# FFN down projection in 1024-column products with seven products for some pairs, and the residual kept in DRAM

## The chip, the cores and the metric

The kernel runs on one core of one Trainium2 chip, in one launch. The metric is device time in microseconds (us) of that core, the median of several runs. TensorE (PE in the profile) multiplies, VectorE (DVE), ScalarE (ACT) and GpSimd (POOL) work elementwise, SyncE (SP) issues most transfers.

## The reference

One layer of a block for 256 tokens of width 2048: RMSNorm, a combined input projection, latent attention and differential attention, gated merge, output projection, and then the part that the change concerns, a SwiGLU feed-forward network (FFN) with a hidden width of 5632 and the final norm. All tensors are float32.

```python
x = x + merged @ w_out[i]
h2 = rmsnorm(x, ffn_norm_g[i])
x = x + (jax.nn.silu(h2 @ w_ffn_gate[i]) * (h2 @ w_ffn_up[i])) @ w_ffn_down[i]
return rmsnorm(x, final_norm_g)
```

## The kernel before

Each float32 operand is split into a high part in float32r and the rest, also in float32r (`split`, L92 a cast on ScalarE, L93 a subtraction on VectorE). A product of two split operands takes three matmuls, high x high, high x low, low x high (`mm3`, L176 to L178), each 128 rows of k by 128 tokens by up to 512 columns. The 256 tokens are two halves h of 128. Weights are loaded from DRAM in pieces of 128 x 2 x 512 (tile raw, six buffers, on SP's queue), split into tiles w (eight buffers) or t (five), and used once. Activations are kept transposed, in tiles L (48 buffers); scratch tiles are s (eight buffers) and n (four).

The output projection runs in four chunks of 512 columns. Each chunk adds x to the product (L593), keeps the sum as the residual x2 in SBUF (eight L tiles until the end), and transposes it (L601) into h2T, the operand of the FFN. For the pairs of k-blocks in SEVEN = (0, 2, 4) `sums_of` also makes h2S, four sums and differences of the pair's four 128 x 128 blocks.

The FFN's 11 hidden chunks of 512 columns go in three parts, of 4, 4 and 3 chunks. `hidden(c, between)` multiplies h2T by 512 gate and 512 up columns over eight pairs of k-blocks. A plain pair takes 8 block products, 24 matmuls. A pair in SEVEN is done in the manner of Strassen and Winograd: `seven_weights` forms sums of the weight blocks (L645 to L647) and splits them, seven block products (21 matmuls) go into PSUM banks 1 to 7, and after the last such pair VectorE and ScalarE combine banks 1, 5, 6 and 7 into four base tiles (L699 to L703). Banks 2, 3, 4 and 8 go on accumulating; at the chunk's end the bases are added to them (L723, L724), and silu and the product with up follow (L726, L727). `between()` is called ahead of pair 6 and transposes the hidden chunk before into banks 5 and 6 (L677), split into fT.

After the hidden chunks of a part its down projection runs, in four chunks of 512 columns, all plain: two banks each, (1, 7) and (2, 3) in turn, accumulated over the part's 16 or 12 k-blocks. The part's last hidden chunk is transposed (`behind()`) ahead of the last four k-blocks of chunk 0. At each chunk's end the two banks are added to x2 (L762). In the last part chunks 0 to 2 are also squared and summed (L244) and multiplied by the final gain, and chunk 3 comes last, its half h=1 in two column halves; after it the row factors are worked out and the rows scaled and stored.

The order of instructions on each engine is set at build time by a scheduler that replays the program against its own clock; on the chip each engine's queue is in order. So neighbouring matmuls can belong to different chunks.

Of the kernel before, what the change touches and what calls it, by code (L numbers as in the profile page):

```python
# [8 lines left out]
F32 = mybir.dt.float32  # L9
# [5 lines left out]
P = 128  # L15
# [23 lines left out]
def hybrid_block(ctx: ExitStack, tc: tile.TileContext, x, xT, gains, w_lat, w_kr, w_dqk, w_dv, w_g0, w_g1, b_gate,  # L39
# [531 lines left out]
    def sums_of(tp, gs):  # L571

        a, t = nt((P, 2, S)), nt((P, 4, P))
        for j in range(2):
            nc.scalar.activation(out=a[:, j], in_=tp[:, j], func=AF.Copy, scale=gs[j])
        a11, a12, a21, a22 = a[:, 0, 0:P], a[:, 1, 0:P], a[:, 0, P:S], a[:, 1, P:S]
        nc.vector.tensor_tensor(out=t[:, 0], in0=a21, in1=a22, op=ALU.subtract)
        nc.vector.tensor_tensor(out=t[:, 1], in0=a11, in1=a21, op=ALU.subtract)
        nc.vector.tensor_tensor(out=t[:, 2], in0=t[:, 0], in1=a11, op=ALU.subtract)
        nc.vector.tensor_tensor(out=t[:, 3], in0=a12, in1=t[:, 2], op=ALU.add)  # L580
        hi, lo = lt(F32R, (P, 4, P)), lt(F32R, (P, 4, P))
        split(t, hi, lo)
        return hi, lo

    x2ss = const.tile([P, 8], F32, name="x2ss")
    for c in range(4):
# [9 lines left out]
        x2.append(z)  # L596
# [64 lines left out]
    def seven_products(q, pair, w, start, stop):  # L661

        hi, lo = h2S[pair]
        s1, s3, s2, s4 = [(hi[:, j], lo[:, j]) for j in range(4)]
        a0, a1 = h2T[2 * pair], h2T[2 * pair + 1]
        ls = {1: part_of(a0, 0), 2: part_of(a1, 0), 3: s4, 4: part_of(a1, 1), 5: s1, 6: s2, 7: s3}
        for i in (1, 5, 7, 6, 2, 3, 4) if start else (1, 3, 2, 5, 7, 6, 4):
            mm3(q[i], ls[i], w[i], start, stop and i in (1, 5, 6, 7))

    def transposed(f, alloc=lt, roles=(5, 6)):  # L670

        res = []
        for i, role in enumerate(roles):
            tp = bank(role, (P, 2, S))
            for j in range(2):
                for h in range(2):
                    nc.tensor.transpose(tp[:, j, h * P:(h + 1) * P], f[h][:, (2 * i + j) * P:(2 * i + j + 1) * P],  # L677
                                        ident)
            hi, lo = alloc(F32R), alloc(F32R)
            split(tp, hi, lo)  # L680
            res += [(hi[:, j], lo[:, j]) for j in range(2)]
        return res

    def hidden(c, between):

        pairs = len(h2T) // 2
        last = max(SEVEN) if SEVEN else None
        q, base = {}, None
        for p in range(pairs):
            if p == pairs - 2:  # L690
                between()
            if p in SEVEN:
                w = seven_weights(w_gu[c, p])
                if not q:
                    q = {i: bank(i) for i in (1, 5, 7, 6, 2, 3, 4)}
                seven_products(q, p, w, p == min(SEVEN), p == last)
                if p == last:
# [8 lines left out]
            g0_, u1, u0, g1_ = plain_weights(w_gu[c, p])  # L706
            if 8 not in q:
                q[8] = bank(8)
            if not SEVEN and not p:
                q.update({i: bank(i) for i in (2, 3, 4)})  # L710
            for a, (wg, wu) in ((h2T[2 * p], (g0_, u0)), (h2T[2 * p + 1], (g1_, u1))):
                first_k = a is h2T[0]
                for h, (i, j) in enumerate(((2, 3), (4, 8))):
                    l = part_of(a, h)
                    end = a is h2T[-1]
                    mm3(q[i], l, wg, first_k, end)
                    mm3(q[j], l, wu, first_k or (j == 8 and SEVEN and p == 1 and a is h2T[2]), end)
# [164 lines left out]
```

## Time and profile before

| | |
|---|---|
| runs, median (lowest to highest) | 1666.11 us (1664.88 to 1667.57), 3 runs |
| profiled execution | 1665.36 us, span in the profile 1663.6 us |
| PE, DVE, ACT, POOL busy | 99%, 70%, 51%, 2% of the span |
| TensorE's granted clock | 0.999 of full speed |
| HBM | 315.9 MB read, 6.3 MB written, 194 GB/s |

Times in the profile are us from the span's start unless marked ns. A busy share says how long an engine was occupied, not whether it set the time; matmuls overlap, so that their durations add up to more than the time that they take. Idle time is put down to what ended it.

### The profile page before, as it was taken

The page shows a single profiled execution, that of the slowest core. Times are in us where ns is not written, and L with a number is a line of the kernel's source. Part 1 is how long each engine was busy: PE and PEld are TensorE (multiplying, and loading weights), DVE is VectorE, ACT ScalarE, POOL GpSimd, SP SyncE. Part 2 cuts the span into 40 slices and gives each one's busy share as a digit, 9 for nine tenths or more (in the row PEclk, how much of TensorE's full clock was granted, in tenths as well). Part 3 has the DMA queues.
Part 4 walks back from the last instruction along what each step waited for, and adds up shares of the span by engine and source line. Part 5 has one row for each costly group of instructions (what it writes and reads, how often), then busy time and mean ns, then how long its engine had stood idle before and what let it go on. Part 6 is the DMA issues. An engine that isn't in the chain of part 4 may idle for free.

```text
span 1663.6 us, 22367 instructions
## 1 busy us (share of the span) xinstructions
PE 1648.0 (99%) x8443; PEld 1407.1 (85%) x8443; DVE 1158.8 (70%) x1490; ACT 845.2 (51%) x1158; POOL 26.2 (2%) x49
## 2 busy tenths in 40 slices
PE   8999999999999999999999999999999999999998
PEld 7888888888888999998888788888888888888886
DVE  7676665666555766765656889975679885688865
ACT  6465554455444666565445555544445554445543
POOL 0000000010000000000000000000000000000010
PEclk9999999999999999999999999999999999999999
DMA  9655555466666545556766566666566655566662
GB/s 329 222 176 168 175 176 178 153 197 203 213 209 197 180 159 176 169 170 207 237 213 207 176 192 197 206 202 202 190 202 202 199 189 196 186 203 203 197 221 103
DMA packets 99133, 323.67 MB, mean 195 GB/s; under 512 B 10960, under 2 KB 17104, under 8 KB 99024
## 3 DMA queue, kind: packets, MB, share of 16 engines
q1 hardware_dynamic: 98880, 322.22, 58.7%
q8 instruction: 66, 1.08, 0.3%
q14 instruction: 43, 0.35, 0.1%
q10 hardware_dynamic: 144, 0.02, 0.0%
HBM read 315.91 MB, written 6.29 MB: 194 GB/s over the span
## 4 chain that ended last, share of the span: by engine, by line
PE 97%; DMA 1%; DVE 1%; ACT 0%; issue 0%; SPq 0%; ACTq 0%; POOLq 0%; POOL 0%; DVEq 0%
PE q L176 14%; PE q L177 14%; PE q L178 14%; PE mm L176 12%; PE mm L177 12%; PE mm L178 12%; PE mm L201 9%; PE mm L202 5%; PE ps L178 1%; PE ps L177 1%; PE ps L176 1%; PE q L677 1%; PE ps L108 1%; DMA raw<-in_w_dqk_dram 1%; DMA raw<-in_w_gu_dram 0%
## 5 line engine op out<-in xcount | busy, mean ns | idle before, releaser
L93 DVE TENSOR_TENSOR wlo<-raw,whi 128x1024 fp32r<-128x1024 f32 (+3 forms) x320 | 381.8, 1194 | 258.1 <-ACT whi L92 252.8
L92 ACT CAST whi<-raw 128x1024 fp32r<-128x1024 f32 (+3 forms) x320 | 329.0, 1028 | 349.0 <-PE mm L177 250.9
L176 PE MATMUL mm<-whi,L 128*128 128x512 f32 (+2 forms) x1080 | 384.0, 358 | 4.7 <-ACT whi L92 4.7
L178 PE MATMUL mm<-whi,L 128*128 128x512 f32 (+2 forms) x1080 | 385.8, 358 | 0.0
L177 PE MATMUL mm<-wlo,L 128*128 128x512 f32 (+2 forms) x1080 | 385.3, 357 | 0.0
L177 PE MATMUL q<-w,L 128*128 128x512 f32 x900 | 350.3, 390 | 0.0
L178 PE MATMUL q<-w,L 128*128 128x512 f32 x900 | 350.0, 390 | 0.0
L92 ACT CAST w<-raw 128x1024 fp32r<-128x1024 f32 x192 | 198.9, 1052 | 262.2 <-PE q L177 254.3
L176 PE MATMUL q<-w,L 128*128 128x512 f32 x900 | 315.0, 390 | 0.3 <-DVE L L96 0.3
L93 DVE TENSOR_TENSOR w<-raw,w 128x1024 fp32r<-128x1024 f32 x192 | 231.7, 1220 | 108.7 <-ACT w L92 108.7
L201 PE MATMUL mm<-L,whi 128*128 128x512 f32 x672 | 240.1, 398 | 0.6 <-DVE n L211 0.6
L176 PEld LDWEIGHTS mm<-whi,L 128*128 128x128 f32 x1080 | 204.3, 190 | 32.8 <-ACT whi L92 4.7
L178 PEld LDWEIGHTS mm<-whi,L 128*128 128x128 f32 x1080 | 204.4, 189 | 28.4
L177 PEld LDWEIGHTS mm<-wlo,L 128*128 128x128 f32 x1080 | 204.4, 189 | 28.3 <-DVE wlo L93 0.5
L176 PEld LDWEIGHTS q<-w,L 128*128 128x128 f32 x900 | 168.8, 188 | 35.2 <-PE q L178 0.7
L178 PEld LDWEIGHTS q<-w,L 128*128 128x128 f32 x900 | 169.0, 188 | 34.9
L177 PEld LDWEIGHTS q<-w,L 128*128 128x128 f32 x900 | 169.0, 188 | 34.6
L202 PE MATMUL mm<-L,wlo 128*128 128x256 f32 x672 | 189.4, 282 | 0.0
L201 PEld LDWEIGHTS mm<-L,whi 128*128 128x128 f32 x672 | 126.2, 188 | 28.5 <-DVE n L211 0.9
L202 PEld LDWEIGHTS mm<-L,wlo 128*128 128x128 f32 x672 | 127.0, 189 | 0.7
L93 DVE TENSOR_TENSOR w<-t,w 128x1024 fp32r<-128x1024 f32 x66 | 79.6, 1218 | 4.6 <-ACT w L92 4.0
L92 ACT CAST w<-t 128x1024 fp32r<-128x1024 f32 x66 | 68.5, 1051 | 25.2 <-PE q L177 12.6
(190 smaller groups left out, 1368.7 us busy)
## 6 DMA issues: line engine op xcount, KB each, us to landing
raw<-in_w_gu_dram SPq DMA_DIRECT2D x176, 512.0 KB, 4.6
raw<-in_w_fd_dram SPq DMA_DIRECT2D x88, 512.0 KB, 4.1
raw<-in_w_dqk_dram SPq DMA_DIRECT2D x64, 512.0 KB, 3.3
raw<-in_w_g_dram SPq DMA_DIRECT2D x64, 512.0 KB, 3.3
raw<-in_w_diff_dram SPq DMA_DIRECT2D x32, 512.0 KB, 3.3
raw<-in_w_mla_dram SPq DMA_DIRECT2D x32, 512.0 KB, 4.0
raw<-in_w_out_dram SPq DMA_DIRECT2D x32, 512.0 KB, 3.7
raw<-in_w_dv_dram SPq DMA_DIRECT2D x30, 512.0 KB, 3.2
```

The costliest lines, as they stand in the source:

```text
L92: nc.scalar.copy(hi, src)
L93: nc.vector.tensor_tensor(out=lo, in0=src, in1=hi.bitcast(F32), op=ALU.subtract)
L108: nc.tensor.transpose(tp[:, j, h * P:(h + 1) * P], blk[h], ident)
L176: nc.tensor.matmul(o, lhsT=l[0], rhs=r[0], start=start, stop=False)
L177: nc.tensor.matmul(o, lhsT=l[0], rhs=r[1], start=False, stop=False)
L178: nc.tensor.matmul(o, lhsT=l[1], rhs=r[0], start=False, stop=stop)
L201: nc.tensor.matmul(o[b], lhsT=ws[k][0][:, bs], rhs=a, start=k == 0, stop=False)
L202: nc.tensor.matmul(o[b][:, :S], lhsT=ws[k][1][:, bs], rhs=ah, start=False, stop=k == len(aT) - 1)
L677: nc.tensor.transpose(tp[:, j, h * P:(h + 1) * P], f[h][:, (2 * i + j) * P:(2 * i + j + 1) * P], ident)
```

## The change

The down projection too goes in chunks of 1024 columns. A new function `product` does what `hidden` did inside, for either operand: n pairs of k-blocks against 1024 columns, pairs in `seven` by seven products, the others plainly, with banks 1, 5, 6, 7 for combined products and 2, 3, 4, 8 for the outputs. `hidden` calls it with h2T and h2S. In parts 0 and 1 the down projection is two products over eight pairs with three seven-product pairs each; in the last part it is one product over six pairs with two such pairs (columns 0 to 1023), then chunk 2 plainly in banks 1 and 7, then chunk 3 as before. `behind()` is called ahead of the last two pairs of a part's first product. For the pairs concerned `transposed` also makes the sums fS of the transposed hidden chunk. `w_ffn_down` is laid out accordingly on the host.

The residual x2 is stored to DRAM in the output projection (eight stores on SP's queue). In parts 0 and 1 base and bank are added and the sum is added to x2 in DRAM by an accumulating transfer issued from POOL (16 of them). In the last part x2 is loaded again (xf, eight loads, with the four rows of the final gain, on POOL's queue), and base and bank are added to it one after the other. The squares of chunks 0 to 2 are taken on ScalarE.

```diff
@@ -570,14 +570,17 @@
 
     def sums_of(tp, gs):
 
-        a, t = nt((P, 2, S)), nt((P, 4, P))
-        for j in range(2):
-            nc.scalar.activation(out=a[:, j], in_=tp[:, j], func=AF.Copy, scale=gs[j])
...
+        a, t = sc((P, 4, P)), sc((P, 4, P))
+        if gs is None:
+            nc.scalar.copy(a.rearrange("p a b -> p (a b)"), tp.rearrange("p a b -> p (a b)"))
+        else:
+            for j in range(2):
+                nc.scalar.activation(out=a[:, 2 * j:2 * j + 2].rearrange("p a b -> p (a b)"), in_=tp[:, j], func=AF.Copy,
+                                     scale=gs[j])
+
+        nc.vector.tensor_tensor(out=t[:, 0:2], in0=a[:, 0:2], in1=a[:, 1::2], op=ALU.subtract)
+        nc.vector.tensor_tensor(out=t[:, 2], in0=t[:, 1], in1=a[:, 0], op=ALU.subtract)
+        nc.vector.tensor_tensor(out=t[:, 3], in0=a[:, 2], in1=t[:, 2], op=ALU.add)
         hi, lo = lt(F32R, (P, 4, P)), lt(F32R, (P, 4, P))
         split(t, hi, lo)
         return hi, lo
@@ -593,7 +596,9 @@
             nc.vector.tensor_add(t, xr, o[h])
             square_sum(t, x2ss[:, 4 * h + c:4 * h + c + 1])
             z.append(t)
-        x2.append(z)
+        x2.append(dram.tile([P, 2, 512], F32, name=f"x2_{c}"))
+        for h in range(2):
+            nc.sync.dma_start(out=x2[c][:, h], in_=z[h])
...
@@ -658,43 +663,25 @@
...
+    def product(aT, aS, n, w, seven, at=None, between=None):
+
+
         q, base = {}, None
-        for p in range(pairs):
-            if p == pairs - 2:
+        outs = (2, 3, 4, 8)
+        for p in range(n):
+            if p == at:
                 between()
-            if p in SEVEN:
-                w = seven_weights(w_gu[c, p])
-                if not q:
-                    q = {i: bank(i) for i in (1, 5, 7, 6, 2, 3, 4)}
-                seven_products(q, p, w, p == min(SEVEN), p == last)
-                if p == last:
+            if p in seven:
+                ws = seven_weights(w(p))
+                fresh = 1 not in q
+                if fresh:
+                    q.update({i: bank(i) for i in (1, 5, 7, 6) + (() if p else outs[:3])})
+                s3, s1, s2, s4 = [(aS[p][0][:, j], aS[p][1][:, j]) for j in range(4)]
+                a0, a1 = aT[2 * p], aT[2 * p + 1]
+                ls = {1: part_of(a0, 0), 2: part_of(a1, 0), 3: s4, 4: part_of(a1, 1), 5: s1, 6: s2, 7: s3}
+                for i in (1, 5, 7, 6, 2, 3, 4) if fresh else (1, 3, 2, 5, 7, 6, 4):
+                    mm3(q[i], ls[i], ws[i], p == 0 if i in outs else fresh, i not in outs and p == max(seven))
+                if p == max(seven):
                     c1, v2, v3, d12, d22 = (sc() for _ in range(5))
                     nc.scalar.copy(c1, q[1])
                     nc.vector.tensor_tensor(out=v2, in0=c1, in1=q[6], op=ALU.add)
@@ -703,66 +690,95 @@
                     nc.vector.tensor_tensor(out=d22, in0=q[5], in1=v3, op=ALU.subtract)
                     base = ((c1, d12), (v3, d22))
                 continue
...
+            b11, b22, b12, b21 = plain_weights(w(p))
+            for k, bs in ((2 * p, (b11, b12)), (2 * p + 1, (b21, b22))):
+                for h in range(2):
+                    for i, b in zip(outs[2 * h:2 * h + 2], bs):
+                        start = i not in q
+                        if start:
+                            q[i] = bank(i)
+                        mm3(q[i], part_of(aT[k], h), b, start, k == 2 * n - 1)
+        return [[(base[h][v] if base else None, q[outs[2 * h + v]]) for v in range(2)] for h in range(2)]
+
+    def transposed(f, seven=False):
+
+        res, sums = [], None
+        for i in range(2):
+            tp = bank(5 + i, (P, 2, S))
+            for j in range(2):
+                for h in range(2):
+                    nc.tensor.transpose(tp[:, j, h * P:(h + 1) * P], f[h][:, (2 * i + j) * P:(2 * i + j + 1) * P],
+                                        ident)
+            if seven and not i:
+                sums = sums_of(tp, None)
+            hi, lo = lt(F32R), lt(F32R)
+            split(tp, hi, lo)
+            res += [(hi[:, j], lo[:, j]) for j in range(2)]
+        return res, sums
+
+    def hidden(c, between):
         f = []
+        for h, ((g_, gq), (u_, uq)) in enumerate(product(h2T, h2S, 8, lambda p: w_gu[c, p], SEVEN, 6, between)):
             sg = nt()
+            nc.vector.tensor_tensor(out=sg, in0=g_, in1=gq, op=ALU.add)
+            nc.vector.tensor_tensor(out=u_, in0=u_, in1=uq, op=ALU.add)
+            nc.scalar.activation(out=sg, in_=sg, func=AF.Silu, scale=r2[:, h:h + 1])
+            nc.vector.scalar_tensor_tensor(out=sg, in0=u_, scalar=r2[:, h:h + 1], in1=sg, op0=ALU.mult, op1=ALU.mult)
             f.append(sg)
         return f
     parts = ((0, 4), (4, 8), (8, 11))
     for i, (a, b) in enumerate(parts):
-        fT, f = [], None
+        fT, fS, f = [], {}, None
+        n = 2 * (b - a)
+        last = i == len(parts) - 1
+        seven = SEVEN[:2] if last else SEVEN
 
         def behind():
             if f:
-                fT.extend(transposed(f))
+                p = len(fT) // 2
+                t, sums = transposed(f, p in seven)
+                fT.extend(t)
+                fS[p] = sums
 
         for c in range(a, b):
             f = hidden(c, behind)
...
+        if last:
+            xf = []
+            for c in range(4):
+                xf.append([lt(shape=(P, 512)) for _ in range(3)])
+                for h in range(2):
+                    nc.gpsimd.dma_start(out=xf[c][h], in_=x2[c][:, h])
+                gf = xf[c][2]
+                nc.gpsimd.dma_start(out=gf, in_=final_norm_g[512 * c:512 * c + 512].unsqueeze(0).broadcast_to([P, 512]))
                 nc.gpsimd.tensor_scalar(out=gf, in0=gf, scalar1=math.sqrt(D), scalar2=None, op0=ALU.mult)
...
+        for cc in range(1 if last else 2):
+            o = product(fT, fS, n, lambda p: w_fd[cc, 2 * a + p], seven, None if cc else n - 2, behind)
             for h in range(2):
-                nc.vector.tensor_add(x2[c][h], x2[c][h], o[h])
-                if last:
-                    square_sum(x2[c][h], fss[:, 4 * h + c:4 * h + c + 1])
-                    nc.vector.tensor_mul(x2[c][h], x2[c][h], x2[c][2])
+                for v, (t, q) in enumerate(o[h]):
+                    c = 2 * cc + v
+                    if last:
+                        nc.vector.tensor_tensor(out=xf[c][h], in0=xf[c][h], in1=t, op=ALU.add)
+                        nc.vector.tensor_tensor(out=xf[c][h], in0=xf[c][h], in1=q, op=ALU.add)
+                    else:
+                        nc.vector.tensor_tensor(out=t, in0=t, in1=q, op=ALU.add)
+                        nc.gpsimd.dma_start(out=x2[c][:, h], in_=t, accum_op=ALU.add)
+    o = [bank(i) for i in (1, 7)]
+    for p in range(n):
+        ws = parts_of(load(w_fd[1, 2 * a + p][:, 0::3]), two)
+        for j in range(2):
+            k = 2 * p + j
+            for h in range(2):
+                mm3(o[h], part_of(fT[k], h), ws[j], k == 0, k == 2 * n - 1)
+    for h in range(2):
+        nc.vector.tensor_add(xf[2][h], xf[2][h], o[h])
+    for c in range(3):
+        for h in range(2):
+            junk = sc()
+            nc.scalar.activation(out=junk, in_=xf[c][h], func=AF.Square, accum_out=fss[:, 4 * h + c:4 * h + c + 1])
+            nc.vector.tensor_mul(xf[c][h], xf[c][h], xf[c][2])
...
+    for p in range(n):
+        raw = load(w_fd[1, 2 * a + p][:, 1:3])
+        for j in (1, 0):
             ws.append((lt(F32R, (P, 512)), lt(F32R, (P, 512))))
-            split(raw[:, j % 2], ws[-1][0], ws[-1][1])
+            split(raw[:, j], ws[-1][0], ws[-1][1])
...
@@ -860,7 +875,9 @@
-    a["w_fd"] = a["w_ffn_down"][0].reshape(NF, 4, P, 4, 512).transpose(3, 0, 2, 1, 4)
+
+    w = a["w_ffn_down"][0].reshape(2 * NF, 2, P, 2, 2, 512).transpose(3, 0, 1, 4, 2, 5)
+    a["w_fd"] = np.stack([w[:, :, i, j] for i, j in ((0, 0), (1, 1), (0, 1), (1, 0))], axis=3)
```

## Rows read from the trace of the kernel before

**Rows 1.** The page: TensorE and VectorE busy, and the chain that ended last.

```profile
PE 1648.0 (99%) x8443; PEld 1407.1 (85%) x8443; DVE 1158.8 (70%) x1490; ACT 845.2 (51%) x1158; POOL 26.2 (2%) x49
...
PE 97%; DMA 1%; DVE 1%; ACT 0%; issue 0%; SPq 0%; ACTq 0%; POOLq 0%; POOL 0%; DVEq 0%
```

**Rows 2.** Waits of TensorE, whole span: us in total, times, longest.

```profile
PE mm L176 <- ACT whi L92: 4.7, 1, 4.7
PE ps L601 <- DVE L L593: 2.0, 2, 1.8
...
PE q L176 <- DVE L L96: 0.3, 1, 0.3
```

**Rows 3.** Timeline of TensorE in a down chunk: start, us, line, operation, names.

```profile
1125.28 0.39 PE L176 MATMUL q<-w,L 128*128 128x512 f32 x1
...
1133.89 0.39 PE L178 MATMUL q<-w,L 128*128 128x512 f32 x1
```

**Rows 4.** Stretches: part 0's hidden chunks, the second of them, its down projection.

```profile
core 0: us, PE busy (x) PEld busy (x) DVE busy (x) ACT busy (x) POOL busy (x), PEclk, DMA share, GB/s
948.00:1117.00 169.00, 168.70 (x757) 139.36 (x756) 144.71 (x166) 91.77 (x106) 1.07 (x3) 1.00 0.61 195
990.00:1032.00 42.00, 42.00 (x191) 34.76 (x190) 38.34 (x44) 24.71 (x28) 0.00 (x0) 1.00 0.63 202
1117.00:1204.00 87.00, 87.00 (x390) 72.04 (x389) 52.39 (x52) 37.77 (x39) 0.00 (x0) 1.00 0.59 197
```

**Rows 5.** Timeline of TensorE around transposes, in a hidden chunk and the down projection.

```profile
1020.80 0.60 PE L677 MATMUL q<-ident,n 128*128 128x128 f32 x4
1021.15 0.48 PE L176 MATMUL q<-w,L 128*128 128x512 f32 x1
...
1025.13 0.60 PE L677 MATMUL q<-ident,n 128*128 128x128 f32 x4
...
1134.12 0.82 PE L677 MATMUL q<-ident,n 128*128 128x128 f32 x6
1134.69 0.71 PE L176 MATMUL q<-w,L 128*128 128x512 f32 x2
```

**Rows 6.** Timeline of VectorE: combining adds and splits of transposed operands.

```profile
1014.94 0.69 DVE L700 TENSOR_TENSOR s<-s,q 128x512 f32<-128x512 f32 x1 [0.93 <-PE q L178]
...
1020.23 0.68 DVE L703 TENSOR_TENSOR s<-q,s 128x512 f32<-128x512 f32 x1
...
1026.38 1.29 DVE L93 TENSOR_TENSOR L<-q,L 128x512 fp32r<-128x512 f32 x2 [0.26 <-ACT L L92]
...
1136.31 1.28 DVE L93 TENSOR_TENSOR L<-q,L 128x512 fp32r<-128x512 f32 x2
...
1314.41 0.69 DVE L700 TENSOR_TENSOR s<-s,q 128x512 f32<-128x512 f32 x1
...
1320.25 0.68 DVE L703 TENSOR_TENSOR s<-q,s 128x512 f32<-128x512 f32 x1
...
1326.06 1.28 DVE L93 TENSOR_TENSOR L<-q,L 128x512 fp32r<-128x512 f32 x2
```

**Rows 7.** Groups by line from 1000 us on: count, busy us, mean ns, idle before.

```profile
L93 DVE TENSOR_TENSOR w<-raw,w 128x1024 fp32r<-128x1024 f32 x180 | 217.2, 1220 | 105.0 <-ACT w L92 105.0
L92 ACT CAST w<-raw 128x1024 fp32r<-128x1024 f32 x180 | 186.5, 1052 | 242.9 <-PE q L177 241.0 <-ACT w L92 1.9
...
L645 DVE TENSOR_TENSOR t<-raw,raw 128x1024 f32<-128x1024 f32 x28 | 34.2, 1223 | 15.3 <-DMA raw<-in_w_gu_dram 15.0
...
L646 DVE TENSOR_TENSOR t<-t,raw 128x512 f32<-128x512 f32 x28 | 19.2, 685 | 0.3
```

**Rows 8.** Waits of all engines in the FFN, 960 to 1655 us.

```profile
DVE t L645 <- DMA raw<-in_w_gu_dram: 15.9, 16, 2.8
```

**Rows 9.** Waits of SP's queue, 900 to 1655 us.

```profile
SPq L624 <- DVE w L93: 481.4, 190, 10.8
```

**Rows 10.** Transfers: issuing queue, count, KB each, median us to landing.

```profile
raw<-in_w_gu_dram SPq DMA_DIRECT2D x176, 512.0 KB, 4.6
...
t<-n SPq DMA_DIRECT2D x8, 256.0 KB, 3.8
```

More of the change, by code (lines that the diff above doesn't have):

```diff
@@ L659, in part_of @@
         return a[0][:, hs], a[1][:, hs]
[L661 to L682, printed above, removed]
@@ L705, in hidden @@
                 continue
[L706 to L717, printed above, removed]
+            b11, b22, b12, b21 = plain_weights(w(p))
@@ L743, in hybrid_block @@
-        for c in range(4):
-            n0 = 512 * c
-            if last:
-                gf = lt(shape=(P, 512))
-                nc.sync.dma_start(out=gf, in_=final_norm_g[n0:n0 + 512].unsqueeze(0).broadcast_to([P, 512]))
-                nc.gpsimd.tensor_scalar(out=gf, in0=gf, scalar1=math.sqrt(D), scalar2=None, op0=ALU.mult)
-                x2[c].append(gf)
-            if last and c == 3:
-                break
-            o = [bank(r) for r in ((1, 7) if c % 2 == 0 else (2, 3))]
-            for m in range(a, b):
-                if not c and m == b - 1:
-                    behind()
-                ws = plain_weights(w_fd[c, m])
-                for j in range(4):
-                    k = 4 * (m - a) + j
-                    for h in range(2):
-                        mm3(o[h], part_of(fT[k], h), ws[j], k == 0, k == 4 * (b - a) - 1)
-            for h in range(2):
-                nc.vector.tensor_add(x2[c][h], x2[c][h], o[h])
-                if last:
-                    square_sum(x2[c][h], fss[:, 4 * h + c:4 * h + c + 1])
-                    nc.vector.tensor_mul(x2[c][h], x2[c][h], x2[c][2])
+        if last:
[6 more added lines that the diff above has]
+                nc.gpsimd.dma_start(out=gf, in_=final_norm_g[512 * c:512 * c + 512].unsqueeze(0).broadcast_to([P, 512]))
+                nc.gpsimd.tensor_scalar(out=gf, in0=gf, scalar1=math.sqrt(D), scalar2=None, op0=ALU.mult)
@@ L773, in hybrid_block @@
     ws = []
[L774 to L777 removed]
+    for p in range(n):
+        raw = load(w_fd[1, 2 * a + p][:, 1:3])
+        for j in (1, 0):
             ws.append((lt(F32R, (P, 512)), lt(F32R, (P, 512))))
[L779 removed]
+            split(raw[:, j], ws[-1][0], ws[-1][1])
     for h in range(2):
         hs = slice(h * P, (h + 1) * P)
[L782 removed]
+        z, y = xf[3][h], lt(shape=(P, 512))
         m = 512 >> h
@@ L799, in hybrid_block @@
         for c in range(4):
-            z = x2[c][h] if c < 3 else y
+            z = xf[c][h] if c < 3 else y
             if c % 2:
```

24 lines of the change are left out of this document (1 added, 23 removed).

## The prediction

> **What bounds the kernel now.** I read the page first. Its busy table and chain [rows 1] put TensorE at 99% of the span, VectorE at 70%, and give the chain that ended last to TensorE for 97%. A busy share by itself doesn't prove a bound, so I looked next at what TensorE waited for [rows 2]: four lines, 7.6 us in the whole span; a window from 960 us to the end has none. So the FFN, from about 948 us to the last matmul some 8 us before the end, is one unbroken stream of matmuls, and its length is their number times their spacing. The spacing is not the 390 ns of the groups, because matmuls overlap: between the two starts of [rows 3] lie 38 matmuls, 8.61 us / 38 = 0.2266 us each. All durations below come from the same execution.
>
> The second engine matters as soon as the first is relieved. By stretches [rows 4] VectorE is busy 38.3 of 42 us in a hidden chunk in mid-part, 144.7 of 169 us in the four hidden chunks of part 0, but only 52.4 of 87 us in the down projection after them. There it catches up.
>
> **The change part by part.**
>
> Products. A pair of k-blocks over 1024 columns costs 2 x 2 x 2 x 3 = 24 matmuls plainly, 7 x 3 = 21 as seven products. Seven products are used for 3 pairs in each of 2 products in parts 0 and 1, and for 2 pairs in the last part: 12 + 2 = 14 pairs, 42 matmuls fewer, 42 x 0.2266 = **-9.5 us**. The rest of TensorE's list stays: transposes, the plain chunk 2, chunk 3 in halves.
>
> The wait at the transposes. The down projection needs the last hidden chunk's transposes in the middle of its first chunk. Before, that cost nothing [rows 5, 6]: six transposes at 1134.12 us, TensorE straight on at 1134.69 with other matmuls, while VectorE finished the new operands only from 1136.31 on. I read the matmuls in between as chunk 1's, since chunk 1 has banks of its own (2 and 3) and weights ready. The new first product holds all eight banks. After its last seven-product pair (p=4 of 8, p=2 of 6) one plain pair is left that needs no new transposes; then come the transposes into banks 5 and 6, and every remaining matmul of the product depends on them. The next product can start only in banks 1 and 7, and its weights stand behind those of the two last pairs. So TensorE must wait. The hidden chunks already run the same sequence, with other matmuls to fill it, so I take its clock from there, counted from the first combining add L700 at 1014.94 us [rows 5, 6]: bank 5 is free when L703 ends, after 6.0 us in that chunk (1020.23 + 0.68); TensorE has finished the plain pair and begins to transpose at 5.9 us (1020.80); four transposes hold it 0.35 us (to 1021.15), eight 0.7 us; from the second batch's start at 1025.13 to the end of the first split (half of 1.29 us after 1026.38) is 1.9 us.
>
> Lower bound: bank 5 is free by 5.9 us, the split is ready at 7.8 us, TensorE's own work lasts until 6.6 us, so it waits about 1.0 us. Upper bound: the slowest chunk from 1314.41 us on [rows 6], where L703 ends 6.5 us after L700 and VectorE reaches the split only at 11.65 us, ready at 12.3: wait about 5.5 us. I take 2.5 us, nearer the low end: in the rows TensorE's filler delayed the second batch, which is gone when TensorE is idle, but one or two weight subtractions of 1.1 us stay between L703 and the split. Three parts, 3 x 2.5 = **+7.5 us** (3.0 to 16.5).
>
> VectorE. A seven-product pair adds one 1024-wide add, two 512-wide adds and one and a half subtractions of 1024 [rows 7]: 1.22 + 2 x 0.69 + 1.22 + 0.69 (the half at the 512-wide price) = 4.5 us, 14 times. Five products add four combining ops each (2.7 us), and eight pairs of transposes get sums: a copy, three small ops and one more split, about 1.6 us of VectorE. In part 0 this is 6 x 4.5 + 2 x 2.7 + 3 x 1.6 = 37 us on top of 144.7 + 52.4 = 197 us within some 252 us: 93% instead of 77%. The hidden chunks ran at 38.3 of 42 without a TensorE wait, so I cost this at 0; the cover is the weights split ahead (eight w tiles, two pairs, 10.9 us of matmuls). If that cover goes, it is the slower rival below. ScalarE, busy 24.7 of 42 us [rows 4], gets one and a half casts more per pair, 1.6 us by the 1.05 us of a full one: 0.
>
> Ends of products. The four adds t+q are as many as a hidden chunk's four L723/L724, after which TensorE did not wait: 0. Their tiles t stay held until the accumulating transfer has read them. No transfer issued from POOL is in the trace. Bounds: below, 0, as these four of the eight s tiles are next wanted by the following combine, five pairs or 111 x 0.2266 = 25 us later, while a store of this size lands in 3.8 us [rows 10]; above, the extra 16 accumulations make weights land later. I take 0. The Trainium skill's page DMA: Bandwidth & Descriptors (Issuing engines are not separate DMA queues) says that transfers from any queue interleave on the same 16 engines. By it the accumulations would push against the weight loads, for whose landing VectorE's L645 already waits 15.9 us in 16 places [rows 8]; that lifts the chance of the slower rival a little and leaves the sum as it is.
>
> Residual stores and loads. Eight 256 KB stores join SP's queue in the output projection; each waits for L593, and behind it stand weight loads. SP waits for freed buffers anyway (481 us in 190 waits [rows 9]) and six raw buffers cover 6 x 2.7 us. The stage's end is the one place without filler: TensorE waited 1.8 us for L593 there [rows 2]. Bounds -1.8 to +1.8, that wait gone or doubled; I take 0. The twelve late loads on POOL's queue have a product of 31 us ahead of their first use; POOL has nothing else queued there but the four scalings. Tail: the six squares of chunks 0 to 2 move to ScalarE and lie beside 16 us of chunk 3's matmuls; what follows the last matmul (8 us) is the same work: 0.
>
> **Sum.** The profiled execution took 1665.36 us with a span of 1663.6: 1665.36 - 9.5 + 7.5 = 1663.4. The median of the runs is 0.75 us higher, so the forecast is **1664.1 us**. A measurement of this kernel can't tell less than 0.2%, 3.3 us, from no change; so my forecast reads as "same".
>
> **Rivals.** *The wait is hidden (faster).* TensorE finds other matmuls at the transposes, or ScalarE and VectorE serve them at once. For it: before, the fill worked, and banks 1 and 7 are free for two of the next product's seven. Against: that product's weights come late. With waits of 0 to 1.0 us the time is 1666.1 - 9.5 + 0 to 3 = 1656.6 to 1659.6; it counts as faster until the three waits reach 6.2 us, 2.1 us each. The Trainium skill's page Perfetto Trace Analysis (Matmul Optimizations) asks that all 8 PSUM banks be used for the most parallelism. By that rule a product over eight banks loses nothing, and the result is this rival's 1656.6; the rows speak against it, since the parallelism that hid the transposes came from a second chain in two spare banks.
>
> *VectorE becomes the bound (slower).* It no longer has the light down projection to catch up. Eight hidden chunks get sums, 1.6 us more VectorE work, while a mid-part chunk has 42 - 38.3 = 3.7 us idle, much of it waits for ScalarE that it can't use. If none can be used, 8 x 1.6 = 12.8 us reach TensorE: 1664.1 + 12.8 = 1676.9; if half, 1670.5. It decides once over 5.3 us of it shows (1664.1 + 5.3 = 1669.4). Against it: no TensorE wait in eleven hidden chunks.
>
> **How the numbers follow.** Forecast case 0.42, hidden wait 0.36, VectorE bound 0.22. The forecast's own range is 1662.8 to 1669.4. For 8 in 10 I reach down to 1657.5, which leaves a tenth of the chances for the full gain, and up to 1671.0, which takes VectorE's half price. Chances: faster 0.36, same 0.42, slower 0.22.
>
> **What would show it.** Right: TensorE waits at the first matmuls after the transposes in the first down product of each part, three places of 1 to 5 us, put down to a split on VectorE or ScalarE, and no other waits in the FFN; 42 matmuls fewer in the q groups at the same 0.227 us. Wrong towards faster: no idle behind those transposes. Wrong towards slower: waits for w or t tiles at pairs with seven products, or landings of weights well over 4.6 us [rows 10]. A different spacing of matmuls, or a longer tail after the last of them, would break the sum elsewhere.

## The result, and the profile after

The changed kernel takes 1686.99 us (median of 4 runs, 1685.19 to 1688.69) beside 1665.77 us of the kernel before on the same chip: ratio 1.0126 [1.0108, 1.0143], 21.2 us slower. The forecast was 1664.1 us with a range up to 1671.0: wrong, and on the far side of the slower rival's worst case, 1676.9. The profiled execution took 1686.71 us, its span 1684.9 us.

The page of the changed kernel: busy time, one DMA queue that was not there before, and the weight loads of the FFN.

```profile
PE 1651.7 (98%) x8401; PEld 1402.9 (83%) x8401; DVE 1232.6 (73%) x1601; ACT 874.9 (52%) x1219; POOL 49.1 (3%) x77
q0 software_dynamic: 3264, 7.34, 2.2%
raw<-in_w_gu_dram SPq DMA_DIRECT2D x176, 512.0 KB, 4.9
raw<-in_w_fd_dram SPq DMA_DIRECT2D x88, 512.0 KB, 4.8
```

The 42 matmuls are gone (8443 before, 8401 now [rows 1]), and TensorE is still the engine that is nearly always busy. The weight loads land in 4.9 us instead of 4.6 [rows 10]; a median over the kernel shows little of what follows.

TensorE's waits from the start of the FFN to its last matmul:

```profile
PE q L177 <- DVE w L93: 8.5, 7, 3.4
PE ps L606 <- DVE L L596: 3.6, 2, 3.5
PE q L176 <- ACT L L92: 3.3, 3, 1.4
PE q L176 <- DVE n L724: 1.8, 2, 1.1
PE q L178 <- DVE L L93: 1.2, 1, 1.2
PE q L710 <- DVE s L690: 0.7, 1, 0.7
```

That is 19.1 us where the same stretch had 2.3 [rows 2]. The six lines are four different troubles: line 1 is mostly the ends of products, line 2 the start of the FFN (L606 is L601 of before), lines 3, 5 and 6 the transposes, line 4 (with short waits of line 1) the ends of hidden chunks. None of them is the whole story.

Waits are not all of it. Below are windows of the same trace; the columns are stretch, its length, busy time and count of PE, PEld, DVE, ACT, POOL, and then the granted clock, the DMA share and GB/s:

```profile
949.00:953.00 4.00, 3.84 (x14) 3.12 (x15) 3.53 (x9) 1.24 (x3) 0.49 (x2) 0.59 0.96 298
1218.00:1224.00 6.00, 6.00 (x28) 4.96 (x27) 3.13 (x4) 3.06 (x3) 0.00 (x0) 1.00 1.03 253
1230.00:1236.00 6.00, 6.00 (x21) 4.78 (x21) 4.46 (x5) 0.83 (x1) 0.00 (x0) 0.75 0.89 239
1495.00:1499.00 4.00, 3.96 (x11) 3.16 (x12) 4.00 (x4) 0.02 (x1) 3.26 (x3) 0.61 1.02 384
```

Behind the three waits of 3 us and more the granted clock is well under 1, and matmuls start 0.43 us apart instead of 0.2266. With seven matmuls behind a fourth wait, of 1.4 us, there are 28 such spacings in the FFN, none before, another 5.5 us. The idle time of a wait also leaves out part of the gap (the 3.03 us below are 3.42 from start to start). Counted from one start to the next, all that is longer than 0.2266 us comes to 33 us between the last matmul of the output projection and the last of the kernel, to 4.8 us before. Less the 9.5 us of matmuls that is 19 us; the starts themselves show the stretch 20.6 us longer (944.58 to 1655.34 us before, 945.05 to 1676.37 now). By place, what is added over the kernel before: ends of products 11.7 us, transposes 8.6, ends of hidden chunks about 6, start of the FFN 2.3.

Now the place that cost most, the end of a part's second down product, on three engines (timelines of VectorE, ScalarE, TensorE).

```profile
1219.91 1.22 DVE L93 TENSOR_TENSOR w<-t,w 128x1024 fp32r<-128x1024 f32 x1
1225.51 1.22 DVE L650 TENSOR_TENSOR t<-raw,raw 128x1024 f32<-128x1024 f32 x1 [4.37 <-DMA raw<-in_w_gu_dram]
1228.10 2.35 DVE L93 TENSOR_TENSOR w<-raw,w 128x1024 fp32r<-128x1024 f32 x2
```
```profile
1220.48 2.00 ACT L92 CAST w<-raw 128x1024 fp32r<-128x1024 f32 x2 [4.03 <-PE q L177]
```
```profile
1225.27 1.07 PE L176 MATMUL q<-w,L 128*128 128x512 f32 x4
1229.37 0.60 PE L177 MATMUL q<-w,L 128*128 128x512 f32 x1 [3.03 <-DVE w L93]
1229.77 0.63 PE L178 MATMUL q<-w,L 128*128 128x512 f32 x1
```

TensorE waits for the low parts of a plain pair's weights. Their high parts were cast by 1222.48, and VectorE had nothing to do from 1221.13 on; but the subtraction stands behind L650, the first addition for the next pair, and that addition waits 4.37 us for its own weights to land. TensorE is charged with a wait for "DVE w"; what was late is a DMA for another pair. The four accumulating transfers of this product's end had been issued from POOL at 1212.75 to 1213.95 us.

### The profile page after: what moved, and what is told of

It reads as the page before. It is cut to its first block, busy times and chain, and to the rows that moved or that the text cites. A ratio compares the mean times of both kernels' runs of the same rounds, so it can differ in the third digit from the quotient of the medians.

```text
span 1684.9 us, 22599 instructions
## 1 busy us (share of the span) xinstructions
PE 1651.7 (98%) x8401; PEld 1402.9 (83%) x8401; DVE 1232.6 (73%) x1601; ACT 874.9 (52%) x1219; POOL 49.1 (3%) x77
## 5 line engine op out<-in xcount | busy, mean ns | idle before, releaser
L177 PE MATMUL q<-w,L 128*128 128x512 f32 x844 | 332.2, 394 | 8.5 <-DVE w L93 8.5
L178 PE MATMUL q<-w,L 128*128 128x512 f32 x844 | 329.2, 392 | 1.3 <-DVE L L93 1.2
L176 PE MATMUL q<-w,L 128*128 128x512 f32 x844 | 282.6, 394 | 3.5 <-ACT L L92 3.3
L92 ACT CAST w<-raw 128x1024 fp32r<-128x1024 f32 x164 | 168.6, 1051 | 201.6 <-PE q L177 180.8
L93 DVE TENSOR_TENSOR w<-raw,w 128x1024 fp32r<-128x1024 f32 x164 | 197.1, 1217 | 17.6 <-ACT w L92 17.5
L177 PEld LDWEIGHTS q<-w,L 128*128 128x128 f32 x844 | 160.0, 190 | 45.2 <-DVE w L93 12.2
L176 PEld LDWEIGHTS q<-w,L 128*128 128x128 f32 x844 | 159.5, 189 | 39.5 <-ACT L L92 4.2
L178 PEld LDWEIGHTS q<-w,L 128*128 128x128 f32 x844 | 159.1, 189 | 34.7 <-DVE L L93 2.2
L92 ACT CAST w<-t 128x1024 fp32r<-128x1024 f32 x94 | 97.5, 1049 | 84.4 <-issue 30.6
L93 DVE TENSOR_TENSOR w<-t,w 128x1024 fp32r<-128x1024 f32 x94 | 113.7, 1223 | 17.9 <-ACT w L92 16.6
```

Source lines behind the costliest of these rows:

```text
L92: nc.scalar.copy(hi, src)
L93: nc.vector.tensor_tensor(out=lo, in0=src, in1=hi.bitcast(F32), op=ALU.subtract)
L176: nc.tensor.matmul(o, lhsT=l[0], rhs=r[0], start=start, stop=False)
L177: nc.tensor.matmul(o, lhsT=l[0], rhs=r[1], start=False, stop=False)
L178: nc.tensor.matmul(o, lhsT=l[1], rhs=r[0], start=False, stop=stop)
```

## The experiments

Two theories at first. A: VectorE's added work comes late in its queue and TensorE pays at the transposes and in hidden chunks. B: the residual's transfers make weights land late. The scheduler replans the order when the program changes; where the order stayed the same it is said.

**1. Down projection plain, residual scheme kept.**

```diff
-        seven = SEVEN[:2] if last else SEVEN
+        seven = ()
...
-                        nc.vector.tensor_tensor(out=t, in0=t, in1=q, op=ALU.add)
+                        t = sc()
+                        nc.vector.tensor_copy(t, q)
```

> All pairs of the down projection are plain, in the same 1024-column products, with the same stores, accumulating transfers and late loads; a copy takes the place of the add of base and bank. It computes the reference. Theory A (VectorE's added work comes late in its queue, and TensorE waits at the transposes): the 42 matmuls come back (+9.5 us), banks 5 and 6 are free so that the transposes can go early, no wait above 0.5 us is left after 960 us; 1664 to 1669 us, level with the kernel before. Theory B (the accumulating transfers and the loads on POOL's queue make weights land late): the waits at the ends of the products stay, 1675 us or more.

1675.38 us, 1.0059 [1.0042, 1.0076]. That is B's number: without any seven-product pair in the down projection the kernel is 9.3 us slower than before. The wait at the start of the FFN is there as in the changed kernel, none is left at transposes, and line 1 of the waits is

```profile
PE q L177 <- DVE w L93: 2.8, 2, 1.6
```

both at the ends of second down products, at 1225 and 1483 us.

**2. The 16 accumulating transfers left out.**

```diff
-                        nc.gpsimd.dma_start(out=x2[c][:, h], in_=t, accum_op=ALU.add)
+                        pass
```

> The 16 accumulating transfers are left out, so that the output lacks the contribution of parts 0 and 1; the adds of base and bank stay. Theory A: at most 2 us faster than the changed kernel, 1685 us; the 3.4 and 3.8 us waits at 1226 and 1491 us stay. Theory B: these waits go with the slow clock behind them, about 10 us, 1677 us.

1675.92 us, 1.0060 [1.0045, 1.0075]: 11 us less than the changed kernel, in the same order on TensorE, VectorE and ScalarE. The waits at the ends of products are nearly gone, those at transposes and in hidden chunks stay. B, for that part.

**3. The sums of the down operands left out** (h2S[0] in their place).

```diff
-                sums = sums_of(tp, None)
+                sums = h2S[0]
```

> The sums of the down projection's left operands are not made; those of the normed input's first pair are used in their place, so that the output is not the reference's. Theory A: the hidden chunks with sums lose their waits (about 1 us in part 0, 2.5 in part 1, 2.3 in part 2, with the slow clock behind them), 1681 us; other waits stay. Theory B: no change, 1687 us.

1675.46 us, 1.0058 [1.0043, 1.0073]: 11.5 us less, more than A asked for. The waits in hidden chunks are gone and those at transposes are shorter; the ends of products keep theirs (3.6 and 2.9 us from start to start). So neither theory alone. The two gains are not two separate causes of equal size, though: by place, in the profiled executions, 6.2 us of this one come from hidden chunks, 1.8 from transposes and 4.0 from the ends of second products, where the waits stayed and 3.2 us of the gain is that no half-clock matmuls follow; small losses elsewhere take 1.5 back.

**4. Two seven-product pairs, transposes ahead of pair 4** of the first product in parts 0 and 1 (12 matmuls more than the changed kernel, 2.7 us).

```diff
-        seven = SEVEN[:2] if last else SEVEN
+        seven = SEVEN[:2]
...
-seven, None if cc else n - 2, behind)
+seven, None if cc else 4, behind)
```

> The down projection takes seven products for the pairs 0 and 2 alone, and the last hidden chunk is transposed ahead of pair 4, so that in parts 0 and 1 two plain pairs (10.9 us of matmuls) lie between the transposes and their use; the last part is as in the changed kernel. It computes the reference. 30 matmuls fewer than before instead of 42 (+2.7 us against the changed kernel). Theory A: the waits at the transposes of parts 0 and 1 go (3.9 and 3.4 us), and VectorE has 18 us less work in four products, so that half of the waits at the products' ends go too: 1687 + 2.7 - 7.3 - 6 = 1676 us. Theory B: the ends of products stay as they are, 1682 us.

1675.41 us, 1.0057 [1.0042, 1.0072]. A's number; the waits at the transposes of parts 0 and 1 are gone. The ends of products cost 3.9 us from start to start instead of 11.7, although all 16 accumulating transfers are there: with one seven-product pair less in most products, and so less work for VectorE, the same transfers do less harm.

**5. The eight residual stores issued from POOL**, the order on TensorE, VectorE and ScalarE unchanged.

```diff
-            nc.sync.dma_start(out=x2[c][:, h], in_=z[h])
+            nc.gpsimd.dma_start(out=x2[c][:, h], in_=z[h])
```

> The eight residual stores of the output projection are issued from POOL instead of SP; the order on TensorE, VectorE and ScalarE is the same. Theory S: the stores wait in SP's queue for the residual add and hold up the weight loads behind them; so the first gate/up weights land late, VectorE's add L596 is late, TensorE waits 3.5 us (1.8 before) at the start of the FFN and runs its next matmuls at half the clock. By it that wait is under 2.2 us here and the time falls by 2 to 4 us, to 1683 to 1685. Rival: the wait comes from VectorE's own order or from the traffic of the stores, wherever they are issued: the wait stays at 3.5 us and the time at 1687.

1685.61 us, 1.0119 [1.0103, 1.0136]; the interval overlaps that of the changed kernel ([1.0108, 1.0143]), so the time settles nothing. The wait at the start fell half way,

```profile
PE ps L606 <- DVE L L596: 2.6, 2, 2.4
```

from 3.5 to 2.4 us, and the half-clock matmuls behind it did not come. Theory S is half right, for about 1 us that the runs can't tell from nothing.

**6. Plain down projection and the residual in SBUF** (as the first, without stores, accumulations and late loads).

```diff
-                        nc.gpsimd.dma_start(out=x2[c][:, h], in_=t, accum_op=ALU.add)
+                        nc.vector.tensor_add(x2[c][h], x2[c][h], q)
```

> All pairs of the down projection plain, as in the first experiment, and the residual kept in SBUF: no stores, no accumulating transfers, no late loads. Theory R: the 9.3 us that the first experiment lost against the kernel before are the residual's path (stores at the start, accumulations at the ends of products): 1666 to 1668 here. Rival: they are the price of 1024-column chunks over banks 2, 3, 4 and 8: 1673 to 1676.

1666.63 us, 1.0005 [0.9995, 1.0014]: no difference from before. The waits in the FFN are back to

```profile
PE ps L604 <- DVE L L596: 1.6, 2, 1.5
PE q L176 <- DVE L L96: 0.3, 1, 0.3
```

(L604 is L606). So 1024-column chunks by themselves cost nothing, and beside plain products the residual's way through DRAM costs 1675.38 - 1666.63 = 8.75 us.

**7 and 8. Residual in SBUF, two seven-product pairs everywhere** (30 matmuls fewer than before, 6.8 us; 50 L tiles; three pairs beside the residual were not run), transposes as in the change (7) or ahead of pair 4 (8, with the edit of the fourth).

> Two pairs with seven products in every down product (30 matmuls fewer than before, 6.8 us), transposes where the change has them, residual kept in SBUF (50 L tiles). If the losses are separate and add up: 1666 minus 6.8 for the matmuls plus about 8 for the transposes plus 4 to 6 in the hidden chunks with sums: 1671 to 1674. If the accumulations were the cause of those waits too, by late weights: 1662 or less. If the waits are VectorE's and grow when the residual's adds come to it (16 more adds of 0.7 us): 1676 or more.

1672.95 us, 1.0040 [1.0025, 1.0055]: in the middle of "separate and add up". The parts differ from what I had put in: from start to start the transposes cost 5.5 us, not 8, and the hidden chunks 6.5, so the number is better than the account behind it.

> As the kernel with two seven-product pairs and the residual in SBUF, but the transposes come ahead of pair 4 of the first down product, so that plain pairs stand between the last seven-product pair and the operands that need them. If the losses are separate: 1666 minus 6.8 plus 4 to 6 (sums in hidden chunks, the last part's transposes): 1662 to 1666. If removing one wait only uncovers another: 1670 or more, no better than the fourth experiment minus 5.

1669.19 us, 1.0018 [1.0008, 1.0027]: 3.8 us better for the transposes, but between the two expectations. Waits behind the third hidden chunk of each part were left (1081, 1333 to 1337, 1591 to 1596 us; in the last part that is already its down product, not its last hidden chunk). From start to start TensorE lost 13.8 us in the FFN, 9.0 more than before, where I had counted on 4 to 6.

**9. The 16 transfers stay, but as plain stores.** The order on every engine is the same as in the changed kernel.

```diff
-                        nc.gpsimd.dma_start(out=x2[c][:, h], in_=t, accum_op=ALU.add)
+                        nc.gpsimd.dma_start(out=x2[c][:, h], in_=t)
```

> The 16 transfers of the changed kernel stay where they are, on POOL's queue, but store their tile in place of accumulating (the output lacks the earlier parts); the order on every engine is the same. Theory W: it is the accumulation, which reads, adds and writes back, that makes the weights behind it land late; with a plain store most of the 11 us of the second experiment are gained: 1677 to 1681, and the waits at the ends of the second down products are under 1 us. Rival: any 256 KB transfer at this place does it, by its traffic or because it is issued from POOL: 1685 to 1688, waits of 3 us or more as in the changed kernel.

1680.36 us, 1.0083 [1.0068, 1.0098]: 6.6 us from one flag. The DMA view of 1205 to 1230 us (packets, MB, share of 16 engines; then size and us to landing), first of the changed kernel:

```profile
q1 hardware_dynamic: 1015, 3.67, 43.2%
q0 software_dynamic: 576, 1.05, 29.0%
raw<-in_w_gu_dram SPq DMA_DIRECT2D x7, 512.0 KB, 6.7
x<-s POOLq DMA_DIRECT2D x4, 256.0 KB, 5.5
```

and with plain stores:

```profile
q1 hardware_dynamic: 1270, 4.61, 60.0%
q0 software_dynamic: 320, 1.05, 12.1%
raw<-in_w_gu_dram SPq DMA_DIRECT2D x8, 512.0 KB, 5.2
x<-s POOLq DMA_DIRECT2D x4, 256.0 KB, 2.5
```

The packets of the same 1.05 MB take 2.4 times as much of the 16 engines' time (29.0 to 12.1%) when they accumulate, the weights beside them land in 6.7 instead of 5.2 us, and the addition L650 that waited 4.37 us above waits

```profile
1220.52 1.22 DVE L650 TENSOR_TENSOR t<-raw,raw 128x1024 f32<-128x1024 f32 x1 [1.39 <-DMA raw<-in_w_gu_dram]
```

TensorE has no wait there any more. One half of the expectation failed: the second such place, at 1483 us, keeps a wait of 4.0 us. There the loads L753 and L755 of the last part run as well (see the fourteenth).

**10. The sums' four operations on POOL** in place of VectorE.

```diff
-        nc.vector.tensor_tensor(out=t[:, 0:2], in0=a[:, 0:2], in1=a[:, 1::2], op=ALU.subtract)
+        e = nc.vector if gs else nc.gpsimd
+        e.tensor_tensor(out=t[:, 0:2], in0=a[:, 0:2], in1=a[:, 1::2], op=ALU.subtract)
...
+        e.tensor_tensor(out=lo, in0=t, in1=hi.bitcast(F32), op=ALU.subtract)
```

> The changed kernel, with the four elementwise operations of the sums of each transposed hidden chunk on POOL in place of VectorE. Theory V: the waits in the last hidden chunk of each part are VectorE's backlog from the sums, so they go, and the time falls by 4 to 8 us, to 1679 to 1683; the waits at transposes and at the ends of products stay. Rival: VectorE is not short of time there, it is the longer hold of banks 5 and 6 by the copy for the sums: the waits stay, and the time is 1685 or more.

1683.68 us, 1.0098 [1.0080, 1.0115]: 3.3 us less, between the two expectations, and the intervals overlap. Undecided by itself. From start to start the three places cost 3.8 us instead of 6.2.

**11. The eighth with the sums and the addition to the residual on POOL.**

> The eighth experiment with the sums' operations and the addition to the residual on POOL in place of VectorE. Theory V: what was left there, 2.6 us of waits above 0.4 us at the start of the last hidden chunk of parts 1 and 2 and smaller ones, is VectorE's backlog: 1664 to 1667, no slower than the kernel before. Rival: removing VectorE's work uncovers waits for weights that land late or for POOL itself: 1669 or more.

1665.62 us, 0.9997 [0.9988, 1.0006]: 3.6 us better than the eighth, as theory V said, here with intervals apart.

**12. As the eleventh, last part with one seven-product pair and its transposes ahead of pair 2.**

```diff
-        seven = SEVEN[:2]
+        seven = SEVEN[:1] if last else SEVEN[:2]
...
-None if cc else 4, behind)
+None if cc else 2 if last else 4, behind)
```

> As the eleventh, and in the last part only one pair with seven products (3 matmuls more, 0.7 us) with the transposes ahead of pair 2, so that two plain pairs stand behind them. If the 1.6 us of waits at the last part's transposes are the late operands, they go: 1 us faster than the eleventh, 1663 to 1666. Rival: they move to the next place where banks change: as the eleventh or up to 1 us slower.

1663.23 us, 0.9981 [0.9972, 0.9990], 2.4 us better than the eleventh: the one version that beats the kernel before, by 3.0 us. From the FFN's start on, its TensorE waits for one thing,

```profile
PE ps L606 <- DVE L L598: 1.9, 2, 1.7
```

which is the wait that the kernel before has too. With 27 matmuls fewer (6.1 us) half of the gain arrives.

**13. The late loads held back** until the last hidden chunk is done.

```diff
+                for t in xf[c]:
+                    nc.gpsimd.tensor_copy(t[:, :1], f[0][:, :1])
```

> The changed kernel, with the twelve loads of the residual and the gain on POOL's queue held back until the last hidden chunk is done (the profile shows them issued from 1480 us on, 150 us ahead of their use). Theory D: there they share the DMA engines with the weights of the last part's first pairs, so the wait of 3.8 us at 1491 us and the slow matmuls behind it are partly theirs: 2 to 5 us faster than the changed kernel, 1682 to 1685, and no new wait at the end. Rival: that wait is the accumulations' alone: 1686 to 1688; or the loads come late for their use and TensorE or the tail waits there: 1688 or more.

1686.40 us, 1.0127 [1.0110, 1.0144]: no change, theory D falls as a matter of time. In the profiled execution the loads go out from 1609 us on, and the wait is moved, not gone: from 1410 to 1670 us its lines are

```profile
PE q L177 <- DVE w L93: 3.2, 3, 2.1
PE q L176 <- ACT L L92: 2.1, 2, 1.4
PE q L178 <- DVE L L93: 1.3, 1, 1.3
PE q L710 <- DVE s L690: 1.2, 1, 1.2
PE q L176 <- DVE n L724: 0.7, 1, 0.7
```

with 2.1 us instead of 3.4 at the end of the product, but the last part's transposes, which waited 0.8 us in the changed kernel, now wait three times (starts up to 1.7 us apart at 1624 to 1630 us). The loads are late there: on VectorE an addition to the residual waits for its tile, and L690, which TensorE's transposes wait for, stands behind it.

```profile
1624.05 0.69 DVE L765 TENSOR_TENSOR L<-L,s 128x512 f32<-128x512 f32 x1 [1.73 <-DMA L<-x]
```

So the rival's second half, loads that come late for their use, is what happened, at a smaller price than it named. The order on TensorE, VectorE and ScalarE is that of the changed kernel.

**14. All three edits to the residual's traffic** (5, 9 and 13 together).

> The three edits to the residual's traffic together: stores of the output projection issued from POOL, plain stores in place of the 16 accumulations (the output lacks the earlier parts), late loads held back. If they add up: 1687.0 - 1.4 - 6.6 - 3 = about 1676, and what is left against the kernel before is what the seven products themselves cost, near the 1673 of the seventh experiment. Rival: the traffic as such still costs: 1679 or more.

1678.77 us, 1.0074 [1.0059, 1.0089]: 8.2 us less than the changed kernel, close to the single gains 1.4 + 6.6 + 0.6 = 8.6, of which only the 6.6 is clear of the noise. The order is that of the changed kernel again. Place by place it is not a sum. At the ends of products no wait is left; the line that stood for them, for the whole kernel, is

```profile
PE q L177 <- DVE w L93: 1.1, 3, 0.4
```

where plain stores alone left 4.0 us at the second such place and held-back loads alone 2.1: there accumulations and early loads share the blame. But the last part's transposes, behind VectorE's wait for a late load as in the thirteenth, cost 5.9 us from start to start instead of 1.3. So the 8.2 us are a gain less a new loss.

## Why the prediction was wrong, step by step

*Products, -9.5 us.* Right in number: 42 matmuls fewer. The spacing of 0.2266 us holds away from waits (28 spacings from 1218.70 to 1225.05 us, 6.35 / 28 = 0.2268). It does not hold right behind some of them, which the sum had not thought of.

*The wait at the transposes, +7.5 us.* The mechanism was right, the places too. In part 0 it comes in three pieces, a wait for L690 (the last combining subtraction, the last to read bank 5) and two for the splits:

```profile
1154.00 0.66 PE L710 MATMUL q<-ident,n 128*128 128x128 f32 x4 [0.69 <-DVE s L690]
1156.00 0.50 PE L176 MATMUL q<-w,L 128*128 128x512 f32 x1 [1.10 <-ACT L L92]
1159.81 0.96 PE L178 MATMUL q<-w,L 128*128 128x512 f32 x3 [1.25 <-DVE L L93]
```

Parts 1 and 2 wait 1.4 and 0.8 us. That is 5.2 us of idle time, and 8.6 us counted from start to start, slow matmuls in part 1 included. The seventh and eighth experiments, whose intervals just touch, put 3.8 us on the transposes of parts 0 and 1. So this term held, though not its lower end (by my own rows 7.8 - 6.6 = 1.2 us a place, not 1.0; the last part has 0.8). The rival that the wait is hidden fell, and with it the rule on eight PSUM banks from which 1656.6 was worked out. That a second chain in spare banks had hidden the transposes fits the sixth experiment, whose plain products leave banks free and wait nowhere there; but it was not tested by itself: the fourth and eighth, with the same eight banks, hid them in parts 0 and 1 by calling them ahead of pair 4, behind one seven-product pair fewer.

*VectorE at 0.* Wrong; the slower rival was right about the engine and wrong about the form. It expected a little in each of eight chunks. What the trace shows is one place in each part, the end of its third hidden chunk, right behind the part's second set of sums; in parts 0 and 1 the fourth chunk follows, in the last part the down product. Behind the first and the third set TensorE does not wait. VectorE in part 0, changed kernel:

```profile
1073.89 0.42 DVE L581 TENSOR_TENSOR s<-s 128x256 f32<-128x256 f32 x1
1075.54 1.23 DVE L650 TENSOR_TENSOR t<-raw,raw 128x1024 f32<-128x1024 f32 x1 [1.23 <-DMA raw<-in_w_gu_dram]
1077.82 0.28 DVE L582 TENSOR_TENSOR s<-s,s 128x128 f32<-128x128 f32 x1
1078.62 0.28 DVE L583 TENSOR_TENSOR s<-s,s 128x128 f32<-128x128 f32 x1
1078.83 0.68 DVE L724 TENSOR_TENSOR n<-s,q 128x512 f32<-128x512 f32 x1
1081.22 0.68 DVE L93 TENSOR_TENSOR L<-s,L 128x512 fp32r<-128x512 f32 x1
```

The sums and their split now stand among the additions that end the chunk. In the kernel before, the first of these additions (its L723) started at 1074.20 us, here (L724) at 1078.83: 4.6 us later, of which 3.1 are the lag of TensorE's whole stream since the start of the FFN. Until these additions are done the banks that the next product wants are held. From start to start this costs 1.1, 2.5 and 2.3 us in the three parts. The sums are not alone in it: in the same place VectorE waits 1.23 us (2.48 and 2.18 us in the other parts) until the weights of L650 land. The cover that I named, weights split ahead, was there on average; it ran out at one place.

*Ends of products and accumulating transfers, 0.* This is the step that failed by most. I had bounded the accumulations by a plain store's landing, and named as the upper bound that they make weights land later, without a price. They did: 6.6 us by the ninth experiment and 11 us by the second, both in the same order of instructions as the changed kernel. They did not do it alone, as far as the runs show: with the same accumulations but fewer or no seven-product pairs, so less work for VectorE, the ends of products cost 3.9 us from start to start (fourth) and 3.5 (first) instead of 11.7. The 0 for VectorE and the 0 here failed together. The Trainium skill's page DMA: Bandwidth & Descriptors (Issuing engines are not separate DMA queues) says that transfers started by any engine interleave on the same 16 engines. The traces agree: the weights on SP's queue landed in 6.7 us beside four accumulations from POOL, in 5.2 us beside four stores.

*Residual stores and late loads, 0.* The stores took the wait at the start of the FFN from 1.8 to 3.5 us, the upper bound that I had given, and matmuls at half clock came behind it; the sixth experiment has 1.5 us without them. (The stores are not needed for the half clock: the twelfth has none of them and has it there too.) The late loads do no harm by being late, but by being early: POOL issues them at 1480 us, into the weights of the last part. Held back they harm another place by about as much. The 31 us of cover that I counted were too many: VectorE adds the bases to the residual as soon as they are combined, from 1622 us on in the changed kernel, some 13 us into the product.

*Tail, 0.* From the last matmul's start to the end 8.2 us before, 8.6 now: right to 0.4 us.

*Rivals.* They were weighed as alternatives, one of which comes true. Three of them came true together, the wait, VectorE's and the DMA's that had no price, and the half-clock matmuls on top. The upper end of 1671.0 was taken from the VectorE rival alone; the forecast's wait plus that rival's full price was already 1676.9.

*What stays open.* The single gains are not separate terms. With 11.5 us for the sums (third) and 8.6 at the transposes they come to 28.3 or 31.2 us, as the traffic is put at 8.2 (fourteenth) or 11.1 (second), of 21.2 + 9.5 = 30.7 us lost. That this is close is partly luck: the third gains at ends of products and transposes too, the fourteenth contains a new loss, and where a part is left out the scheduler may order the rest anew. In the third that includes ScalarE's copy for the sums, which also keeps a bank of the transposes longer; the tenth keeps the copy and moves VectorE's operations alone, for 3.3 us that are not clear of the noise. So how the 11.5 us divide between VectorE's time, the hold of the bank and the new order was not separated. In its own kernel the eleventh measures 3.6 us for two sums per part and the additions to the residual together. Executions of kernels with such waits also spread more (1682.85 to 1689.23 us in the thirteenth) than those of the kernel before, so single profiles tell places better than sizes.

## What to carry to other kernels

A matmul stream without waits lives on its slack: before a few per cent of its matmuls are saved, ask of every engine and of the DMA what the slack at the tightest place is, not on average, and add the mishaps up instead of choosing among them. A wait that the profile puts down to an engine is followed to that engine's own queue: here VectorE was idle with ready work behind an instruction whose data was still in flight. And an accumulating transfer is not a store; where the sum had room in SBUF, adding there was much the cheaper way to keep it (on VectorE in the sixth experiment, on POOL in the eleventh and twelfth).

## What the runs showed of the hardware that I had not expected

The packets of four accumulating transfers took 2.4 times as much of the 16 DMA engines' time as those of four plain stores of the same 1.05 MB, and landed in 5.5 instead of 2.5 us each (ninth experiment).

After TensorE had stood still for 3.0 to 3.5 us in the changed kernel its granted clock averaged 0.59, 0.75 and 0.61 in the windows above, where five, eight and eight matmuls start about 0.43 us apart, the lower of the two levels. So a wait can cost half as much again: at 1226 us it was 3.0 us of idle time and about 1.6 us in the eight matmuls behind it. Whether the clock falls doesn't follow from the wait's length alone. In the third experiment TensorE stood still for 3.2 us at the same place, and the window behind has the full clock:

```profile
1229.00:1235.00 6.00, 5.79 (x25) 4.80 (x26) 5.81 (x7) 1.79 (x3) 0.00 (x0) 1.00 0.65 184
```

At the transposes of part 1 two starts lie 1.94 or 1.95 us apart in the changed kernel, in the ninth experiment and in the thirteenth; seven such spacings follow in the first and in the last, none in the ninth:

```profile
1414.00:1420.00 6.00, 5.46 (x23) 4.18 (x24) 3.65 (x6) 0.43 (x1) 0.00 (x0) 1.00 0.84 242
```

That is the window of the ninth behind its wait, at full clock; the changed kernel has there

```profile
1419.00:1425.00 6.00, 4.55 (x13) 3.49 (x13) 5.35 (x7) 2.05 (x4) 0.00 (x0) 0.72 0.64 169
```

Even the version that beats the kernel before has eight such matmuls behind its wait of 1.7 us at the start of the FFN; the kernel before has none behind its 1.8 us. The half clock is one reason, though not shown to be the only one, why executions of a kernel with waits differ by several us.
